# Keeping K's partial sums in PSUM over the whole first stage, and projecting B of the first SSD groups behind it

## The chip, the cores and the metric

The kernel runs on one core of one Trainium2 chip. The metric is the device time of one execution in microseconds. A time is given as the median of several runs; 0.2% of this kernel's time is 3.5 us.

Five engines matter: PE (TensorE, the matrix products), ACT (ScalarE), DVE (VectorE), POOL (GpSimd) and SP, whose queue here does nothing but start DMA transfers. Each engine takes its instructions strictly in the order of its own queue. An instruction that waits holds up all that stand behind it on its engine. PE writes its results into eight PSUM banks of 128x512 fp32.

## The reference

Two layers of a diffusion backbone on 256 latent tokens and 256 context tokens of width 2048. The even layer, with which the program starts:

```python
shift, scale, gate = adaln(c, ada_w[i], ada_b[i])              # silu(c) @ w + b
h  = modulate(rms_norm(x, norm_g[i]), shift, scale)            # h * (1 + scale) + shift
hc = modulate(rms_norm(ctx, norm_g[i]), shift_c, scale_c)      # the same with c_ctx
p  = h @ w_in                    # columns Q, gate G, Z, K, V, X, B, C, dt
pc = hc @ w_in[:, base:]         # of the context only K, V, X, B, C, dt
ya = neighbourhood_attention(q, k, v, k_ctx, v_ctx, rpb) * silu(gate)
yb = gated_group_rmsnorm(bidirectional_ssd(x, B, C, dt) + d * x, z, ssm_norm_g)
x  = x + gate * (concat([ya, yb]) @ w_out)
```

The odd layer is a gated short convolution between two projections. All products have fp32 accuracy: an operand is split into a high part (hH of the activations, H of a weight) and the low rest (hL, L), both rounded for the fast product type, and each product is three: hH·H, hL·H, hH·L.

## The kernel before, in words

The kernel is built by a Python program that writes all instructions in one order of its own. `Plan` keeps a modelled time for each engine. Pieces of work are Python generators that `spawn` puts into one of three lists (urgent, side, back); `pump` is called between the products of a stage and lets such a piece emit its next instructions when its inputs are modelled as ready; `force` emits pieces until a condition holds. So a change of buffers changes the order on all engines, and the hardware then runs each engine's queue in exactly that order.

**The first stage** (`for j in range(8)`) works through the contraction of 2048 in eight blocks j of 256. For block j it needs h of these rows, which needs the norm of x (row tiles 0 to 3: two of latent, two of context tokens, held in `x0` to `x3`), its transposes (`xm0` to `xm15`, two for each block, through a PSUM bank), and adaLN of the block: `A` (part 0, scale) and `S` (part 1, shift). A part is four loads of 0.5 MB from `ada0` and 16 small products (32x256); in blocks 4, 5 and 7 part 1 is made by DVE dot products instead (`csb<-raw,full`). From A, S and xm come `hH` on ACT (line 780) and `hL` on DVE (lines 786 and 792).

With h(j) the stage projects the first four heads: K (4 row tiles x 2 x 3 = 24 products), V (24), Q (2 row tiles, 12), each 128x512; and B of the first two SSD groups (12 products, into `psB0`). Q and B add up in PSUM over all eight blocks (2 + 2 banks). K and V don't: each row tile of each block gets a bank for six products and then `part_gen` takes it out, by an ACT copy in block 0 (line 816) and a DVE add into SBUF later (line 818): K into `gt` and `sz` (`parK`), V into `Vt`.

In block 0 the row tiles come one after another, since x arrives so: K, V and Q of tiles 0 and 1, then K and V of tile 2, then K and V of tile 3. `h(0, 3)` is the first block's h for tile 3, and needs the transposes of x3.

**Weights** come through five staging places `raw0` to `raw4` (and `PT`, `xtm`, `yi`, idle memory in this stage). A load is issued on SP by `issue` as soon as a place is free, in the order of `loads`. `split` then makes the high part on ACT (`w0` to `w2`, or `wH`, line 422) and `low_part` the low one on DVE (line 429). There are three weight places; `splits_try` emits a cast when a place is free and the weights are modelled to be there at most 300 ns behind the engines' time.

After the stage come G and dt, and `do_ssd(0)`: C, X, Z of the first two groups, then the attention of the first heads and so on.

Of the kernel before, what the change touches and what calls it, by code (L numbers as in the profile page):

```python
# [9 lines left out]
F32R = mybir.dt.float32r  # L10
# [131 lines left out]
def kernel(ctx: ExitStack, tc, x, cx, ada0, w0, adaT, w_in, w_out, sc_in, sc_out, rpb, small, const,  # L142
# [12 lines left out]
    def st(shape, tag, dt=F32, name=None):  # L155
        return sb.tile(list(shape), dt, tag=tag, name=name or tag, bufs=1)
# [21 lines left out]
    sz, xtm, yi = st([128, 4, 256], "sz"), st([128, 2, 512], "xtm"), st([128, 4, 256], "yi")  # L178
    PTs = st([128, 2, 4, 256], "PT")
    PT = [PTs[:, k] for k in range(2)]  # L180

# [27 lines left out]
    def spawn(q, gen, tmps=0, halves=0, late=0):  # L209
        q.append(Task(gen, tmps, halves, late))  # L210
# [192 lines left out]
    def split():  # L403
        k = pos["split"]
# [74 lines left out]
    def used():  # L479
        pos["use"] += 1  # L480
        w = in_use.popleft()
        if w is not None:
            free_w.append(w)
        splits_try()


# [318 lines left out]
    statk, statq = st([128, 16], "statk"), st([128, 8], "statq")  # L805


    szf, gtf = sz.rearrange("p a b -> p (a b)"), gt.rearrange("p a b -> p (a b)")
    parK = [szf[:, 0:512], szf[:, 512:1024], gtf[:, 0:512], gtf[:, 512:1024]]
    parV = [Vt[:, t, :] for t in range(4)]  # L810

    def part_gen(j, key, t, o, p):
# [107 lines left out]
            mm(ps, hH[kb][:, tt], HLo[1][:, k], False, last and k == 1)  # L920
            pump()

    pars = {"K": parK, "V": parV}

    def kv(j, key, t, HLo):
# [4 lines left out]
    def b_part(j):  # L930
        H, Lo = use()
        for k in range(2):
            mm_ws(psB0, hH[2 * j + k], hL[2 * j + k], H[:, k], Lo[:, k], 512, j == 0 and k == 0, j == 7 and k == 1)
        used()

    for j in range(8):
        need[0] = j
        if j == 1:
            plan.RATE = 360.0
        force(lambda: ("h", j, 0 if j == 0 else 3) in got, (urgent,) if j == 0 else (urgent, side))  # L940
        if j == 0:

            w3 = [use(k) for k in range(3)]
            psQ = banks(2)
            psk = banks(2)
            for k in range(2):

                for i, (a_, w_) in enumerate(((hH, 0), (hL, 0), (hH, 1))):
                    for t in range(2):
                        mm(psk[t], a_[k][:, t * 128:(t + 1) * 128], w3[0][w_][:, k], k == 0 and i == 0, k == 1 and i == 2)  # L950
            for t in range(2):
                spawn(urgent, part_gen(j, "K", t, parK[t], psk[t]))
            pump()
            for t in range(2):
                kv(j, "V", t, w3[1])
            for t in range(2):
                rows_(j, "Q", t, psQ[t], w3[2], True, False)
            for t in range(2, 4):
                force(lambda: ("h", j, t) in got, (urgent,))
                if t == 3:  # L960

                    free_w.append(in_use[2])
                    in_use[2] = None
                    splits_try()
                for key, k in (("K", 0), ("V", 1)):
                    kv(j, key, t, w3[k])
            for k in range(3):
                used()
            psB0 = banks(2)
            b_part(j)  # L970
        else:
            for key in "KVQ":
                HLo = use()
                for t in range(2 if key == "Q" else 4):
                    if key == "Q":
                        rows_(j, key, t, psQ[t], HLo, False, j == 7)
                    else:
                        kv(j, key, t, HLo)
                used()
            b_part(j)  # L980
    force(lambda: all(("part", 7, key, t) in got for key in "KV" for t in range(4)), (urgent,))
    plan.RATE = Plan.RATE
    KT, KL = st([128, 4, 512], "KT", F32R), st([128, 4, 512], "KL", F32R)


    cwh = st([128, 160], "cwh")
# [628 lines left out]

    Btm[0] = st([128, 2, 4, 128], "Btm", name="Btmt")
    spawn(urgent, first_v())
    spawn(urgent, kq_gen("K", 0, parK, 4, statk, KT, KL, False), 4)
    spawn(urgent, kq_gen("Q", 0, psQ, 2, statq, QT, QL, True), 2)

    def do_g(a, nxt, leave=False):
        psG = banks(2)
        proj(512, 256, psG, nxt, leave)
        spawn(urgent, silu2_gen("G", a, psG, gt, lambda: attn[0] >= 8 * a and (a or ("K", 0) in got)), 1)

    def do_ssd(s, nxt):
        if s:
            psB = banks(2)
            proj(256, 512, psB, 1)
            spawn(urgent, make_b(s, psB), 3)  # L1630
        psC, = banks(1)
        proj(256, 256, [psC], 4)
        spawn(urgent, make_c(s, psC), 0, 2)
        psX = banks(4)
        proj(512, 512, psX, 2)
        for gi in range(2):
# [3 lines left out]
        spawn(urgent, silu2_gen("Z", s, psZ, sz, lambda: ssd_done[0] >= 2 * s and ("K", 0) in got), 1)  # L1640
# [580 lines left out]
```

## Time and profile before

| | |
|---|---|
| runs | 1739.43, 1741.1, 1741.53 us; median 1741.1 |
| profiled execution | span 1738.3 us; its own time is not listed apart, and the three runs lie 1.1 to 3.2 us above this span |
| PE busy | 1717.7 us (99%) |
| weight loads into PE (PEld) | 1451.5 us (84%), beside the products |
| DVE busy | 1253.3 us (72%) |
| ACT busy | 776.2 us (45%) |
| granted PE clock | 9 tenths or more in all slices |
| memory traffic | 391.03 MB, mean 225 GB/s |
| first product of block 0 to 7 on K | 23.06, 52.73, 76.45, 95.09, 114.28, 133.45, 156.26, 173.90 us |
| end of the stage | about 190.4 us |

How to read it: a kernel whose PE is busy for 99% of the span gains only by fewer products or by fewer of the few waits that are left; it loses by each microsecond that PE stands. The first stage is where DMA is dense: its first three slices of 43 us move 375, 366 and 319 GB/s. In the lists below, "idle before <- X" or "X <- Y: a, b, c" says that work on X stood for a us in total, b times, c us at the longest, until Y was done. In a list in order of time, the first number is the start and the second the length, and "x2" two such instructions, which overlap.

### The profile page before, as it was taken

How to read it: one execution, taken by the hardware profiler on the slowest of the kernel's cores; microseconds unless marked ns; L12 is line 12 of the kernel's file. 1: busy time of each engine (PE TensorE's matmuls, PEld its weight loads, DVE VectorE, ACT ScalarE, POOL GpSimd, SP SyncE). 2: the span in 40 equal slices, each digit the busy share in tenths (PEclk: the TensorE clock that was granted, in tenths of full speed). 3: DMA queues.
4: the chain of work that ended last, by engine and by line, in shares of the span. 5: the costliest groups of instructions: out<-in, count | busy, mean ns of one | idle time of the engine just before them, and what ended most of it. 6: DMA issues, size and time to landing. Idle time of an engine off the chain costs nothing.

```text
span 1738.3 us, 24820 instructions
## 1 busy us (share of the span) xinstructions
PE 1717.7 (99%) x9255; PEld 1451.5 (84%) x9255; DVE 1253.3 (72%) x2108; ACT 776.2 (45%) x1367; POOL 33.2 (2%) x28
## 2 busy tenths in 40 slices
PE   6999999999999999999999999999999999999999
PEld 4777989889888889888888898888888888888887
DVE  5698787877576877676877687887668667665654
ACT  6434544445243445243435243665445344444442
POOL 0000100001000001000000000000000000000000
PEclk9999999999999999999999999999999999999999
DMA  9987644566754765755766567767867888776763
GB/s 375 366 319 271 206 135 142 180 209 187 228 183 151 234 210 183 227 188 164 230 221 195 191 196 248 258 225 254 280 204 260 267 272 284 246 241 191 248 213 114
DMA packets 192391, 391.03 MB, mean 225 GB/s; under 512 B 16200, under 2 KB 45960, under 8 KB 192016
## 3 DMA queue, kind: packets, MB, share of 16 engines
q1 hardware_dynamic: 184960, 382.88, 67.8%
q10 hardware_dynamic: 7312, 6.59, 1.2%
q8 instruction: 72, 1.18, 0.3%
q14 instruction: 47, 0.39, 0.1%
HBM read 379.79 MB, written 9.62 MB: 224 GB/s over the span
## 4 chain that ended last, share of the span: by engine, by line
PE 96%; DMA 2%; DVE 2%; issue 0%; SPq 0%; ACT 0%; POOL 0%; DVEq 0%; ACTq 0%
PE bank L196 93%; PE bank L200 3%; DMA raw<-in_ada 1%; DMA full<-dram_crow 1%; DVE csb L859 0%; DVE w L429 0%; DVE raw L859 0%; SPq L603 0%; DVE gt L818 0%; DVE yi L859 0%; DVE tmp L623 0%; DVE hL L792 0%; DVE sz L818 0%; DVE tmp L2116 0%; SPq L383 0%
## 5 line engine op out<-in xcount | busy, mean ns | idle before, releaser
L422 ACT CAST w<-raw 128x1024 fp32r<-128x1024 f32 (+1 forms) x344 | 359.8, 1047 | 554.7 <-PE bank L196 462.0
L429 DVE TENSOR_TENSOR w<-raw,w 128x1024 fp32r<-128x1024 f32 (+1 forms) x344 | 417.2, 1216 | 239.5 <-ACT w L422 238.2
L196 PE MATMUL bank<-hH,w 128*128 128x256 f32 (+1 forms) x2064 | 487.0, 325 | 0.0
L196 PE MATMUL bank<-w,hH 128*128 128x512 f32 x1280 | 405.7, 396 | 4.0 <-ACT hH L780 2.5
L196 PEld LDWEIGHTS bank<-hH,w 128*128 128x128 f32 x2064 | 345.3, 188 | 32.1 <-issue 1.7
L196 PE MATMUL bank<-hL,w 128*128 128x256 f32 (+1 forms) x1040 | 335.0, 322 | 0.0
L196 PEld LDWEIGHTS bank<-w,hH 128*128 128x128 f32 x1280 | 237.1, 188 | 56.3 <-DVE gt L818 3.4
L196 PE MATMUL bank<-w,hL 128*128 128x512 f32 x640 | 250.0, 391 | 0.2
L196 PEld LDWEIGHTS bank<-hL,w 128*128 128x128 f32 x1040 | 196.5, 189 | 14.5
L196 PE MATMUL bank<-w,h 128*128 128x512 f32 x768 | 178.2, 390 | 0.0
L196 PEld LDWEIGHTS bank<-w,h 128*128 128x128 f32 x768 | 144.1, 188 | 29.7
L888 DVE CUSTOM_DVE_ANT_0 raw<-raw,csb 128x1024 f32<-128x1024 f32 x128 | 155.3, 1218 | 11.9 <-DMA raw<-in_adaT 9.1
L196 PEld LDWEIGHTS bank<-w,hL 128*128 128x128 f32 x640 | 120.2, 188 | 25.7 <-DVE hL L792 0.9
L196 PE MATMUL bank<-w,mix 128*128 128x512 f32 x588 | 137.8, 391 | 0.0
L196 PEld LDWEIGHTS bank<-w,mix 128*128 128x128 f32 x588 | 109.7, 188 | 22.2 <-issue 0.3
L1371 DVE SCALAR_TENSOR_TENSOR tmp<-bank,cwh,tmp 128x508 f32<-128x508 f32 (+1 forms) x96 | 71.3, 746 | 1.9
L196 PE MATMUL bank<-KL,h 128*128 128x512 f32 x264 | 63.9, 390 | 0.0
L196 PEld LDWEIGHTS bank<-KL,h 128*128 128x128 f32 x264 | 49.5, 188 | 10.2
L196 PE MATMUL bank<-wH,h 128*128 128x512 f32 x168 | 55.7, 391 | 0.0
L196 PE MATMUL bank<-QT,h 128*128 128x512 f32 x168 | 55.7, 391 | 0.0
L429 DVE TENSOR_TENSOR wL<-raw,wH 128x1024 fp32r<-128x1024 f32 x31 | 37.9, 1223 | 23.9 <-ACT wH L422 23.8
L429 DVE TENSOR_TENSOR QL<-raw,QT 128x1024 fp32r<-128x1024 f32 x32 | 39.1, 1223 | 22.1 <-ACT QT L422 21.8
(306 smaller groups left out, 1962.3 us busy)
## 6 DMA issues: line engine op xcount, KB each, us to landing
raw<-in_w_in SPq DMA_DIRECT2D x196, 512.0 KB, 3.8
raw<-in_adaT SPq DMA_DIRECT2D x128, 512.0 KB, 4.8
raw<-in_sc_in SPq DMA_DIRECT2D x128, 512.0 KB, 4.7
raw<-in_w_out SPq DMA_DIRECT2D x64, 512.0 KB, 4.5
raw<-in_ada SPq DMA_DIRECT2D x35, 512.0 KB, 7.7
raw<-in_sc_out SPq DMA_DIRECT2D x32, 512.0 KB, 4.7
raw<-in_w SPq DMA_DIRECT2D x16, 512.0 KB, 5.5
tmp<-dram_csr SPq DMA_DIRECT2D x32, 256.0 KB, 5.2
```

The source lines that it names most:

```text
L196: E(T.matmul(o, l, r, start=start, stop=stop, skip_group_check=True))
L200: E(T.transpose(o, i, ident if k == 128 else ident[:k, :k]))
L422: E(S.copy(H, v))
L429: E(V.tensor_tensor(out=Lo, in0=v, in1=H.bitcast(F32), op=ALU.subtract))
L888: E(V.tensor_tensor_reduce(out=raw, in0=raw, in1=csb, scale=1.0, scalar=0.0, op0=ALU.mult, op1=ALU.add, accum_out=gp[:, h, m:m + 1]))
L1371: E(V.scalar_tensor_tensor(out=do, in0=di, scalar=cwh[:, 32 * k + ch:32 * k + ch + 1], in1=do, op0=ALU.mult, op1=ALU.add))
```

## The change

1. K gets four PSUM banks (`psK`) for the whole stage, its products add up there over all blocks; no copies, no adds. `kq_gen("K", ...)` later reads the banks.
2. That leaves two banks for V's partial sums (still taken out block by block), adaLN and the transposes of x; `psB0` no longer exists.
3. B is not projected in the stage. `do_ssd(0)` projects it as all later groups' B, from loads in full size (four of 0.5 MB instead of eight of 0.25 MB).
4. The memory of `gt` and `sz` is free until the stage ends and becomes a fourth weight place `wH3`/`wL3`, for the first 24 splits.
5. From block 1 on, K and V are projected row tile by row tile in turn, not K whole and then V.

```diff
-    QT, Vt, gt = st([128, 4, 256], "QT", F32R), st([128, 4, 512], "Vt"), st([128, 4, 256], "gt")
+    QT, Vt = st([128, 4, 256], "QT", F32R), st([128, 4, 512], "Vt")
+    WH.append(st([128, 1024], "gt", F32R, name="wH3"))
...
+    WL.append(st([128, 1024], "sz", F32R, name="wL3"))
...
-    free_w, in_use = deque(range(NW)), deque()
+    free_w, in_use = deque(range(NW + 1)), deque()
+    NFIRSTW = 24
+
+    def free_place():
+        return next((w for w in free_w if w != NW or pos["split"] < NFIRSTW), None)
 
     def place():
-        in_use.append(free_w.popleft())
-        return in_use[-1]
+        w = free_place()
+        free_w.remove(w)
+        in_use.append(w)
+        return w
...
-        while free_w and pos["split"] in RAW:
+        while free_place() is not None and pos["split"] in RAW:
...
-    weight(w_in, 0, 2, COL_B, 256)
...
-        weight(w_in, j * 256, 2, COL_B, 256)
...
-    for j_ in ssd_cols(0)[1:]:
+    for j_ in ssd_cols(0):
...
+    psK = []
+
+    def v_rows(j, t, HLo):
         ps, = banks(1)
-        rows_(j, key, t, ps, HLo, True, True)
-        spawn(urgent, part_gen(j, key, t, pars[key][t], ps))
+        rows_(j, "V", t, ps, HLo, True, True)
+        spawn(urgent, part_gen(j, "V", t, parV[t], ps))
+
+    def k_rows(j, t, HLo):
+        if j == 0:
+            psK.extend(banks(1))
+        rows_(j, "K", t, psK[t], HLo, j == 0, j == 7)
...
-            psB0 = banks(2)
-            b_part(j)
         else:
...
-            b_part(j)
+            HK = use()
+            for t in range(4):
+                k_rows(j, t, HK)
+                if t == 0:
+                    HV = use(1)
+                v_rows(j, t, HV)
+            used()
+            used()
+            HQ = use()
+            for t in range(2):
+                rows_(j, "Q", t, psQ[t], HQ, False, j == 7)
+            used()
...
-    spawn(urgent, kq_gen("K", 0, parK, 4, statk, KT, KL, False), 4)
+    spawn(urgent, kq_gen("K", 0, psK, 4, statk, KT, KL, True), 4)
...
     def do_ssd(s, nxt):
-        if s:
-            psB = banks(2)
-            proj(256, 512, psB, 1)
-            spawn(urgent, make_b(s, psB), 3)
+        psB = banks(2)
+        proj(256, 512, psB, 1)
+        spawn(urgent, make_b(s, psB), 3)
...
-    spawn(urgent, make_b(0, psB0), 3)
```

Over the whole program PE has 8849 matrix instructions in the order before and after. SP has 833 loads and stores instead of 837, DVE 28 adds (K) fewer, ACT four copies fewer.

The change also moves the order at the end of block 0, where row tile 3 is made ready. In the lists, a row is an instruction, by line, operation, output and inputs, and shape; numbers behind names are buffer numbers; line numbers after the change are higher by up to 8. On ACT, from the scaling of x3 on, before:

```order
L633 ACTIVATE x3_199<-x3_199,rx_153 128x512 x2
L816 COPY Vt_100<-bank7_89 128x512
L648 COPY xm0_137<-bank3_85 128x128
L648 COPY xm2_139<-bank1_83 128x256
L780 ACTIVATE hH0_297<-xm0_137,S0_155,A0_154 128x128
L780 ACTIVATE hH1_304<-xm1_138,S0_155,A0_154 128x128
L747 COPY half2_76<-bank0_82 128x256
```

and after:

```order
L641 ACTIVATE x3_199<-x3_199,rx_153 128x512 x2
L822 COPY Vt_100<-bank0_82 128x512
L430 CAST wH3_101<-raw1_91 128x1024
L656 COPY xm0_137<-bank3_85 128x128
L656 COPY xm2_139<-bank2_84 128x256
L656 COPY xm4_141<-bank0_82 128x256
L788 ACTIVATE hH0_297<-xm0_137,S0_155,A0_154 128x128
L788 ACTIVATE hH1_304<-xm1_138,S0_155,A0_154 128x128
L755 COPY half2_76<-bank2_84 128x256
```

The cast of block 1's K weights has come ahead of the copy of x3's transposes; before, the cast `w0_95<-raw3_93` of the same weights stood sixteen rows behind that copy.

On SP, the loads behind the constants, before (`in_w_in` is B of block 0, `in_ada0` adaLN, `in_w0` the K and V weights of block 1):

```order
L385 DMA raw2_92<-in_w_in 128x2x256
L383 DMA raw3_93<-in_ada0 128x1024
L383 DMA raw4_94<-in_ada0 128x1024
L383 DMA PT_107<-in_ada0 128x1024
L383 DMA xtm_105<-in_ada0 128x1024
L383 DMA yi_106<-in_ada0 128x1024
L383 DMA PT_107<-in_ada0 128x1024
L383 DMA raw0_90<-in_ada0 128x1024
L383 DMA raw1_91<-in_ada0 128x1024
L383 DMA raw3_93<-in_w0 128x1024
L383 DMA raw4_94<-in_w0 128x1024
```

and after:

```order
L385 DMA raw2_92<-in_ada0 128x1024
L385 DMA raw3_93<-in_ada0 128x1024
L385 DMA raw4_94<-in_ada0 128x1024
L385 DMA PT_107<-in_ada0 128x1024
L385 DMA xtm_105<-in_ada0 128x1024
L385 DMA yi_106<-in_ada0 128x1024
L385 DMA PT_107<-in_ada0 128x1024
L385 DMA raw0_90<-in_ada0 128x1024
L385 DMA raw1_91<-in_w0 128x1024 x2
L385 DMA raw2_92<-in_ada0 128x1024
```

B's load is gone and each adaLN load has moved to another place; the K and V weights of block 1 both go into raw1, where V's waits until K's is split.

On PE, behind the first transposes of x3 (`cpad` marks adaLN products, and the first rows of each list are transposes), before:

```order
L200 MATMUL bank1_83<-const_110,x2_196 128x128
L200 MATMUL bank1_83<-const_110,x3_199 128x128
L196 MATMUL bank0_82<-raw3_93,cpad_112 32x256 x4
L196 MATMUL bank0_82<-raw4_94,cpad_112 32x256 x4
L196 MATMUL bank0_82<-PT_107,cpad_112 32x256 x4
L196 MATMUL bank0_82<-xtm_105,cpad_112 32x256 x4
```

and after:

```order
L202 MATMUL bank0_82<-const_110,x2_196 128x128
L202 MATMUL bank0_82<-const_110,x3_199 128x128
L198 MATMUL bank3_85<-w0_95,hH0_297 128x512
L198 MATMUL bank3_85<-w0_95,hL0_301 128x512
L198 MATMUL bank3_85<-w0_95,hH0_297 128x512
L198 MATMUL bank2_84<-raw2_92,cpad_112 32x256 x4
L198 MATMUL bank2_84<-raw3_93,cpad_112 32x256 x4
```

The first three K products of row tile 3, which need hH0 and hL0 of h(0, 3), have come ahead of block 1's adaLN products.

More of the change, by code (lines that the diff above doesn't have):

```diff
@@ L483, in used @@
             free_w.append(w)
+        if pos["use"] == NFIRSTW:
+            free_w.remove(NW)
         splits_try()
@@ L805 @@
     statk, statq = st([128, 16], "statk"), st([128, 8], "statq")
-    szf, gtf = sz.rearrange("p a b -> p (a b)"), gt.rearrange("p a b -> p (a b)")
-    parK = [szf[:, 0:512], szf[:, 512:1024], gtf[:, 0:512], gtf[:, 512:1024]]
     parV = [Vt[:, t, :] for t in range(4)]
@@ L921, in rows_ @@
             pump()
-    pars = {"K": parK, "V": parV}
-    def kv(j, key, t, HLo):
+    psK = []
+    def v_rows(j, t, HLo):
         ps, = banks(1)
-        rows_(j, key, t, ps, HLo, True, True)
-        spawn(urgent, part_gen(j, key, t, pars[key][t], ps))
[L930 to L934, printed above, removed]
+        rows_(j, "V", t, ps, HLo, True, True)
[4 more added lines that the diff above has]
+        rows_(j, "K", t, psK[t], HLo, j == 0, j == 7)
     for j in range(8):
@@ L944 @@
             psQ = banks(2)
-            psk = banks(2)
+            psK += banks(2)
             for k in range(2):
@@ L949 @@
                     for t in range(2):
-                        mm(psk[t], a_[k][:, t * 128:(t + 1) * 128], w3[0][w_][:, k], k == 0 and i == 0, k == 1 and i == 2)
-            for t in range(2):
-                spawn(urgent, part_gen(j, "K", t, parK[t], psk[t]))
+                        mm(psK[t], a_[k][:, t * 128:(t + 1) * 128], w3[0][w_][:, k], k == 0 and i == 0, False)
             pump()
             for t in range(2):
-                kv(j, "V", t, w3[1])
+                v_rows(j, t, w3[1])
             for t in range(2):
@@ L964 @@
                     splits_try()
-                for key, k in (("K", 0), ("V", 1)):
-                    kv(j, key, t, w3[k])
+                k_rows(j, t, w3[0])
+                v_rows(j, t, w3[1])
             for k in range(3):
                 used()
-            psB0 = banks(2)
-            b_part(j)
-        else:
[L972 to L979, printed above, removed]
-            b_part(j)
-    force(lambda: all(("part", 7, key, t) in got for key in "KV" for t in range(4)), (urgent,))
+        else:
+            HK = use()
[10 more added lines that the diff above has]
+            used()
+    force(lambda: all(("part", 7, "V", t) in got for t in range(4)), (urgent,))
     plan.RATE = Plan.RATE
     KT, KL = st([128, 4, 512], "KT", F32R), st([128, 4, 512], "KL", F32R)
+    gt, sz = st([128, 4, 256], "gt"), st([128, 4, 256], "sz")
     cwh = st([128, 160], "cwh")
@@ L1623, in do_g @@
         proj(512, 256, psG, nxt, leave)
-        spawn(urgent, silu2_gen("G", a, psG, gt, lambda: attn[0] >= 8 * a and (a or ("K", 0) in got)), 1)
+        spawn(urgent, silu2_gen("G", a, psG, gt, lambda: attn[0] >= 8 * a), 1)
     def do_ssd(s, nxt):
-        if s:
-            psB = banks(2)
-            proj(256, 512, psB, 1)
-            spawn(urgent, make_b(s, psB), 3)
+        psB = banks(2)
+        proj(256, 512, psB, 1)
+        spawn(urgent, make_b(s, psB), 3)
         psC, = banks(1)
@@ L1639, in do_ssd @@
         proj(512, 256, psZ, nxt)
-        spawn(urgent, silu2_gen("Z", s, psZ, sz, lambda: ssd_done[0] >= 2 * s and ("K", 0) in got), 1)
+        spawn(urgent, silu2_gen("Z", s, psZ, sz, lambda: ssd_done[0] >= 2 * s), 1)
         for gi in range(2):
             spawn(side, group_gen(s, gi), 4, 4, 3000)
-    spawn(urgent, make_b(0, psB0), 3)
     do_g(0, 1)
```

2 lines of the change are left out of this document (1 added, 1 removed).

## The prediction, as put on record before the changed kernel ran

> **What bounds the kernel now.** I read the page's busy line and chain first, then the windows, then the waits of TensorE (PE) inside the first stage, 23.06 us (first product) to 190.4 us.
>
> ```profile
> PE 1717.7 (99%) x9255; PEld 1451.5 (84%) x9255; DVE 1253.3 (72%) x2108; ACT 776.2 (45%) x1367; POOL 33.2 (2%) x28
> PE 96%; DMA 2%; DVE 2%; issue 0%; SPq 0%; ACT 0%; POOL 0%; DVEq 0%; ACTq 0%
> ...
> 0.00:20.00 20.00, 8.92 (x86) 5.91 (x90) 9.90 (x33) 10.09 (x23) 1.31 (x6) 1.00 0.91 351
> 20.00:40.00 20.00, 16.65 (x112) 11.00 (x101) 13.87 (x37) 14.97 (x32) 1.98 (x4) 1.00 1.04 400
> 40.00:60.00 20.00, 20.00 (x172) 14.24 (x173) 11.51 (x28) 9.01 (x20) 0.00 (x0) 1.00 0.96 358
> 23.06:190.40 167.34, 163.59 (x984) 122.65 (x985) 129.91 (x236) 74.56 (x132) 1.98 (x4) 1.00 0.86 312
> ...
> PE bank L196 <- ACT hH L780: 2.5, 2, 1.4
> PE bank L196 <- DVE gt L818: 1.5, 3, 0.7
> PE bank L200 <- ACT half L747: 0.4, 1, 0.4
> PE bank L200 <- ACT x L633: 0.3, 1, 0.3
> ```
>
> PE works 1717.7 of 1738.3 us and carries 96% of the chain. A window's row gives length, then busy us of PE, weight loads, DVE, ACT and POOL, granted clock, DMA share, GB/s. In the stage PE lacks 3.75 of 167.34 us; the waits name 4.7 us, nearly all that any edit of the stage could give back. And to 60 us the stage lives on a full memory path: 351, 400, 358 GB/s.
>
> **The change part by part.** *PE.* The number of products is the same. What a product costs is read from a stretch without waits:
>
> ```profile
> 80.42 0.62 PE L196 MATMUL bank<-w,hH 128*128 128x512 f32 x2
> 80.87 0.39 PE L196 MATMUL bank<-w,hL 128*128 128x512 f32 x1
> 81.10 0.62 PE L196 MATMUL bank<-w,hH 128*128 128x512 f32 x2
> ```
>
> Three products from 80.42 to 81.10: 0.227 us each, three 0.68. B's 12 products a block are 2.72 us, 8 blocks 21.8 us. They leave the stage and come back whole in do_ssd(0), in the same stationary form. PE waits nowhere there that the list shows, so this is 0 on the path; what it does is take 2.72 us of cover out of each block. Bounds: 1.0 better (every B transition free) to 2.7 worse (one block's B not hidden behind the weights' arrival); I take 0, the groups' rows are alike.
>
> *The adds of K.* They are 28 on DVE:
>
> ```profile
> L818 DVE TENSOR_TENSOR gt<-gt,bank 128x512 f32<-128x512 f32 x14 | 9.5, 682 | 0.7 <-PE bank L196 0.7
> L818 DVE TENSOR_TENSOR sz<-sz,bank 128x512 f32<-128x512 f32 x14 | 9.2, 683 | 2.1 <-PE bank L196 2.0
> L859 DVE CUSTOM_DVE_ANT_0 csb<-raw,full 128x1024 f32<-128x1024 f32 x7 | 8.5, 1220 | 0.9 <-DMA raw<-in_ada 0.9
> ```
>
> 18.7 us of DVE work and four ACT copies go, off the path except for the 1.5 us that PE waited on adds into gt. With the 0.4 us on a half copy I count 1.9 us back (between 0 and 4.7, all waits listed). What may replace them are V's adds: with K and Q parked in six banks only two banks turn over, and an add now may stand behind dot products (1220 ns each); that is a rival below.
>
> *The splits of B.* Eight half-size casts and low parts become four whole ones, eight loads of 0.26 MB four of 0.52 MB, all on the same queues, later. The page's GB/s by slices of 43 us, as far as the place where B now stands (the fifth and after):
>
> ```profile
> GB/s 375 366 319 271 206 135 142 180 209 187 228 183 151 234 210 183 227 188 164 230 221 195 191 196 248 258 225 254 280 204 260 267 272 284 246 241 191 248 213 114
> ```
>
> 206, 135 and 142 where 400 was reached earlier: room for two more loads, ACT and DVE likewise. I take 0; bounds 0.3 better (the half copy's waits go) and 1.4 worse (the longest wait of the list, for a cast instead of hH).
>
> *The fourth weight place and SP's queue.* This decides. The order under the change shows ACT's row: CAST wH3<-raw1, the first half of block 1's K weights, stands in front of the copy xm0<-bank3 that takes row tile 3's transposes from PE. On SP its load is row 26, behind the eight adaLN loads of block 1. What the queues did then:
>
> ```profile
> 21.94 0.38 SPq L385 DMA_DIRECT2D raw<-in_w_in  x1
> 24.83 2.72 SPq L383 DMA_DIRECT2D raw<-in_ada  x2
> 31.60 1.61 SPq L383 DMA_DIRECT2D raw<-in_ada  x2
> 38.75 0.80 SPq L383 DMA_DIRECT2D raw<-in_w  x2
> ...
> GB/s 412 402 412 410 410 410 410 410 399 398 398 423 399 430 399 430 379 430 389 440 379 430 410 338 225 113 369 399 440 379 461 369 410 399 399 430 410 410 430 389
> ...
> DMA to landing us min/median/max: 4.3/6.8/7.6
> ```
>
> (SP's issues; the GB/s of 30 to 46 us in slices of 0.4; the landings of line L383 from 24 to 46 us, of which the least, 4.3, is K1's: issued 38.75, landed 43.05.) K1 was issued only when PE had freed raw3 at 38.7, and the memory path ran dry meanwhile: 338, 225, 113 GB/s from 39.2 to 40.4, which is 1.65 slices' worth, so all that was issued ahead ended near 39.2 + 1.65 x 0.4 = 39.9. In the changed kernel K1 goes to raw1, free early, and follows the adaLN loads without the gap; B's 0.26 MB is not ahead of it (0.26/0.41 = -0.6), its own 0.52 MB is (+1.3): last byte at 40.5. Before, the path picked up at 40.4 and K1's landing came 2.6 later for 1.3 us of bytes, so 1.3 more: 41.8. I take 41.5, bounds 40.5 and 42.4. Now ACT and DVE there:
>
> ```profile
> 36.47 1.34 ACT L633 ACTIVATE x<-x,rx 128x512 f32<-128x512 f32 x2 [0.27 <-POOL rx L592]
> 37.72 0.56 ACT L816 COPY Vt<-bank 128x512 f32<-128x512 f32 x1
> 38.18 0.54 ACT L648 COPY xm<-bank 128x128 f32<-128x128 f32 x2
> 38.60 0.89 ACT L780 ACTIVATE hH<-xm,S,A 128x128 fp32r<-128x128 f32 x2
> ...
> 48.68 2.00 ACT L422 CAST w<-raw 128x1024 fp32r<-128x1024 f32 x2
> ...
> 38.48 0.70 DVE L649 COPY xm<-bank 128x128 f32<-128x128 f32 x2 [0.49 <-ACT xm L648]
> 39.09 0.34 DVE L786 TENSOR_SCALAR tmp<-xm,A,S 128x128 f32<-128x128 f32 x1
> 39.54 0.29 DVE L792 TENSOR_TENSOR hL<-tmp,hH 128x128 fp32r<-128x128 f32 x1
> 49.76 2.36 DVE L429 TENSOR_TENSOR w<-raw,w 128x1024 fp32r<-128x1024 f32 x2
> ```
>
> ACT is through with Vt at 38.2 and now stands until 41.5. The cast takes 1.05 (2.00 for two, overlapping), so xm0 is copied from 42.55 instead of 38.18, xm2 and xm4 follow, and hH0 is there at 43.9. DVE copies xm1, xm3, xm5 after ACT's copies, then does the low part of K1 (1.2, half of 2.36) ahead of row tile 3's: hL0 at 45.6. Queued on PE behind hH0 are the products that follow, in order:
>
> ```profile
> 37.25 0.88 PE L200 MATMUL bank<-const,x 128*128 128x128 f32 x6 [0.30 <-ACT x L633]
> 38.05 1.07 PE L196 MATMUL bank<-raw,cpad 128*32 128x256 f32 x16
> 50.87 0.64 PE L196 MATMUL bank<-PT,cpad 128*32 128x256 f32 x8
> 52.73 0.50 PE L196 MATMUL bank<-w,hH 128*128 128x512 f32 x1
> ```
>
> Before, PE went from the transposes straight into adaLN of block 1 (38.05), which needs nobody but DMA. Now the first three K products of tile 3 stand ahead of it, and the transposes have two more pairs: they end near 38.7. PE then waits
>
> - for hH0 from 38.7 to 43.8: 5.1;
> - for hL0 from 44.1 to 45.6: 1.5;
> - at V of tile 3, whose bank holds xm8: ACT, 4.4 late, has hH1, two half copies, xm6 and V's cast (1.05) ahead of that copy: 1.0;
> - at the first K products of block 1: DVE has V's low part (1.2) ahead of the sums S from which hH2 and hL2 are made: 1.1.
>
> Sum 8.7 us, in a stretch where it waited for nothing (20.00 of 20 busy). Bounds: with K1 at 40.5 the first wait is 4.1 and the last two may vanish, 5.6 in all; with 42.4 it is 6.0 and 9.6. I take 8.7, since adaLN work (1.86 a part, 50.87 to 52.73) no longer lies in the gap. It can't be given back: block 1 on is PE at 99%.
>
> **Sum**: 1738.3 + 8.7 - 1.9 + 0 = 1745.1 us of span. The runs lie 1.1 to 3.2 above the profiled span, their median 2.8; 1745.1 + 2.8 = 1747.9, so 1748.0, or +6.9.
>
> [...] At the start of the program the same transposes run at two speeds (rows from 10 to 14.1 us, and from 14.3 to 16.8):
>
> ```profile
> L200 PE MATMUL bank<-const,x 128*128 128x128 f32 x7 | 1.7, 421 | 0.0
> L200 PE MATMUL bank<-const,x 128*128 128x128 f32 x25 | 3.0, 276 | 0.0
> ```
>
> 421 ns and then 276, 1.7/7 = 0.24 us against 3.0/25 = 0.12 of busy time each. A cold PE is thus half as fast here, though the granted clock reads 1.00. A second cold start after the 5.1 us wait would double the products of the next 3.7 us (first PE work near 10.5 to 14.2) and cost 1.9. [...]
>
> **Rivals.** *Faster*: K1 lands before ACT asks. ACT asks at 38.2, so 3.3 us earlier than I have it; then no wait arises and the listed ones go: 1741.1 - 1.9 = 1739, at best 1741.1 - 4.7 = 1736.4. Against it: the path is at 400 GB/s from 20 to 40, it would have to carry 3.3 x 0.41 = 1.35 MB more, and only B's 0.26 MB was taken off. It decides at a landing of 38.2 and is half gone at 40.
>
> *About the same*: K1 lands at 40.5 or sooner and the last two waits are absorbed by the work around them: PE's waits 5.6, less 1.9, and less up to 2.8 if the rest of the listed waits goes too: +0.9 to +3.7, some 1743.
>
> *Two banks*: V's add waits behind three dot products and a split on DVE: 3 x 1.22 + 1.22 + 0.68 = 5.6 us, while PE, with two banks, can go on for V, K, V products, 3 x 1.37 = 4.1: 1.5 us lost at each such place, three to six of them: +4.5 to +9 on my sum, 1752 to 1757. For it: DVE is 129.91 of 167.34 busy. Against: 18.7 us of that goes away with K's adds.
>
> *Cold clock*: +1.9 on the sum, 1749.9.
>
> That the change doesn't move what it says is excluded: the order shows the adds gone and B's products behind the stage.
>
> **How the numbers follow.** Forecast 0.50; cold clock 0.12; two banks 0.13; about the same 0.17; faster 0.08. Slower is the first three, 0.75. 0.2% is 3.5 us, about what the runs (2.1 us apart) can tell from nothing. 1740 to 1754 leaves out the faster case (0.08), a little of the same case, and a third of the two-bank case.
>
> **What would show it.** ACT idle some 3.3 us near 38 for a load of raw<-in_w; PE's waits on line L788 (hH) grow from 2.5 to about 7, and there is a PE gap of 5 us at 38.7; adds of V alone, 28, and none into gt or sz; block 1's first K product near 55.7 instead of 52.73; the stage's end, now without B, near 190.4 - 21.8 + 6.8 = 175.4. I am wrong if ACT's cast of wH3 starts before 39.5, if PE's wait there is under 3 us, or if waits on the V adds come to over 3 us.

## The result: 14.6 us slower, and the profile after

The changed kernel took 1754.39 to 1756.76 us, median 1754.9, against 1739.43 to 1741.53, median 1740.3, for the kernel before in the same sessions. The ratio is 1.0086, 95% interval 1.0074 to 1.0098. The direction was forecast, the +6.9 was about half of it, and 1754.9 lies above the range of 1740 to 1754. The profiled execution has a span of 1752.6 us and a time of 1754.39, so times stand 1.8 above spans; the difference of the profiled spans is 14.3.

The page's first lines, and PE's waits from 23 to 200 us:

```profile
PE 1721.2 (98%) x9255; PEld 1451.4 (83%) x9255; DVE 1237.1 (71%) x2076; ACT 773.9 (44%) x1359; POOL 31.4 (2%) x28
...
PE bank L198 <- ACT hH L788: 6.7, 3, 4.2
PE bank L198 <- DVE hL L800: 1.8, 2, 1.1
PE bank L198 <- DVE Vt L824: 1.1, 1, 1.1
PE bank L198 <- DVE A L763: 1.0, 1, 1.0
PE bank L198 <- DVE xm L657: 0.9, 1, 0.9
PE bank L202 <- ACT half L755: 0.5, 1, 0.5
PE bank L198 <- DVE wL L437: 0.3, 1, 0.3
```

In the stage, up to Q's last product, PE's idle time went from 3.75 to 11.33 us. The wait for gt is gone, as it must be; the wait for hH grew from 2.5 to 6.7, and five that were not there came: for hL, for V's adds, for adaLN's sums (A), for xm and for the low part of a weight, 5.1 us together. ACT and PE at the place that the prediction spoke of:

```profile
39.19 0.56 ACT L822 COPY Vt<-bank 128x512 f32<-128x512 f32 x1
42.47 1.04 ACT L430 CAST wH<-raw 128x1024 fp32r<-128x1024 f32 x1 [2.73 <-DMA raw<-in_w]
43.42 0.81 ACT L656 COPY xm<-bank 128x128 f32<-128x128 f32 x3
44.11 0.89 ACT L788 ACTIVATE hH<-xm,S,A 128x128 fp32r<-128x128 f32 x2
...
39.80 0.66 PE L202 MATMUL bank<-const,x 128*128 128x128 f32 x4 [0.20 <-ACT Vt L822]
44.67 0.79 PE L198 MATMUL bank<-w,hH 128*128 128x512 f32 x1 [4.22 <-ACT hH L788]
46.58 0.80 PE L198 MATMUL bank<-w,hL 128*128 128x512 f32 x1 [1.12 <-DVE hL L800]
47.74 2.79 PE L198 MATMUL bank<-raw,cpad 128*32 128x256 f32 x24
56.09 0.50 PE L198 MATMUL bank<-w,hH 128*128 128x512 f32 x1 [0.92 <-DVE xm L657]
58.37 0.50 PE L198 MATMUL bank<-wH,hH 128*128 128x512 f32 x1
59.58 0.50 PE L198 MATMUL bank<-wH,hL 128*128 128x512 f32 x1 [0.72 <-DVE hL L800]
```

ACT stands 2.73 us for K1's load, then casts, then copies x3's transposes; PE stands 4.22 us for hH, 1.12 for hL, 0.92 for xm8's bank, and 0.72 for hL behind block 1's first K product. These four were forecast at 5.1, 1.5, 1.0 and 1.1. That first K product starts at 58.37, forecast near 55.7. And 24 adaLN products from 47.74 on take 2.79 us; by the prediction's row of 16 in 1.07 they would take some 1.6. The windows say why. They are cut at the points where the granted clock changes; the number behind POOL's is the clock:

```profile
40.52:43.93 3.41, 0.00 (x0) 0.00 (x0) 0.21 (x1) 1.46 (x4) 0.00 (x0) 1.00 0.06 25
43.93:47.34 3.41, 1.55 (x3) 0.79 (x3) 3.05 (x8) 1.07 (x4) 0.00 (x0) 0.50 0.12 37
47.34:50.76 3.42, 3.42 (x34) 1.39 (x32) 0.00 (x0) 0.00 (x0) 0.00 (x0) 0.50 0.55 204
50.76:54.17 3.41, 3.41 (x45) 2.09 (x41) 0.92 (x4) 1.69 (x3) 0.00 (x0) 1.00 0.83 243
```

Behind a window without a product the clock is 0.50 for two windows of 3.41 us. And far behind the stage, in the output projection, PE waits twice where it had waited for nothing (ACT, then PE):

```profile
1146.24 0.37 ACT L1258 COPY half<-bank 128x256 f32<-128x256 f32 x1 [2.77 <-PE bank L198]
1148.47 2.94 ACT L430 CAST w<-raw 128x1024 fp32r<-128x1024 f32 x3
...
1149.56 0.49 PE L198 MATMUL bank<-w,mix 128*128 128x512 f32 x1 [1.68 <-ACT w L430]
1150.82 2.57 PE L198 MATMUL bank<-w,mix 128*128 128x512 f32 x10 [0.77 <-DVE w L437]
```

Three casts of w_out stand on ACT behind a copy that waits for the attention's products; PE waits 2.4 us.

The account of the profiled spans: first product 23.06 to 24.52, +1.5; idle time in the stage +7.6; halved clock, by the busy time in its two windows, at most (1.55 + 3.42)/2 = 2.5; idle time in the tail +2.4. Sum 14.0 of 14.3. The first product's 1.5 is not the change's: before_tail below, whose program is the same up to there as the kernel before, had it at 24.60. How much of it stands in the medians is not shown.

### The profile page after: what moved, and what is told of

The parts are those of the page before. It is cut to its first block, busy times and chain, and to the rows that moved or that the text cites. A ratio compares the mean times of both kernels' runs of the same rounds, so it can differ in the third digit from the quotient of the medians.

```text
span 1752.6 us, 24755 instructions
## 1 busy us (share of the span) xinstructions
PE 1721.2 (98%) x9255; PEld 1451.4 (83%) x9255; DVE 1237.1 (71%) x2076; ACT 773.9 (44%) x1359; POOL 31.4 (2%) x28
## 4 chain that ended last, share of the span: by engine, by line
PE 95%; DMA 2%; DVE 2%; ACT 1%; issue 0%; SPq 0%; DVEq 0%; ACTq 0%
PE bank L198 92%; PE bank L202 3%; DMA full<-dram_crow 1%; DMA raw<-in_ada 0%; DVE csb L865 0%; DMA raw<-in_w 0%; DMA xtm<-in_w 0%; DVE w L437 0%; ACT hH L788 0%; DVE wL L437 0%; DVE Vt L824 0%; DVE hL L800 0%; ACT wH L430 0%; SPq L611 0%; ACT w L430 0%
## 5 line engine op out<-in xcount | busy, mean ns | idle before, releaser
L437 DVE TENSOR_TENSOR w<-raw,w 128x1024 fp32r<-128x1024 f32 x340 | 414.5, 1222 | 263.8 <-ACT w L430 258.1
L430 ACT CAST w<-raw 128x1024 fp32r<-128x1024 f32 x340 | 357.5, 1053 | 545.9 <-PE bank L198 477.6
L198 PE MATMUL bank<-w,hH 128*128 128x512 f32 x1200 | 382.4, 396 | 9.7 <-ACT hH L788 6.7
L198 PEld LDWEIGHTS bank<-w,hH 128*128 128x128 f32 x1200 | 222.1, 188 | 57.5 <-ACT hH L788 7.4
L198 PE MATMUL bank<-w,hL 128*128 128x512 f32 x600 | 234.3, 391 | 1.2 <-DVE hL L800 1.1
L198 PEld LDWEIGHTS bank<-hL,w 128*128 128x128 f32 x1040 | 196.2, 189 | 14.6
L198 PEld LDWEIGHTS bank<-w,hL 128*128 128x128 f32 x600 | 112.7, 188 | 25.4 <-DVE hL L800 2.2
L437 DVE TENSOR_TENSOR wL<-raw,wH 128x1024 fp32r<-128x1024 f32 x35 | 42.8, 1222 | 23.6 <-ACT wH L430 23.6
L430 ACT CAST wH<-raw 128x1024 fp32r<-128x1024 f32 x36 | 37.9, 1052 | 45.3 <-PE bank L198 34.6
L437 DVE TENSOR_TENSOR QL<-raw,QT 128x1024 fp32r<-128x1024 f32 x32 | 39.1, 1223 | 24.8 <-ACT QT L430 24.7
L198 PE MATMUL bank<-wH,h 128*128 128x512 f32 x168 | 55.7, 390 | 0.0
```

The costliest lines, as they stand in the source:

```text
L198: E(T.matmul(o, l, r, start=start, stop=stop, skip_group_check=True))
L430: E(S.copy(H, v))
L437: E(V.tensor_tensor(out=Lo, in0=v, in1=H.bitcast(F32), op=ALU.subtract))
```

## The experiments

Theory 1: the early cast on ACT, with its load behind a full memory path, is the price. Theory 2: two working banks are. Theory 3: B's products were cover (work of PE during which other engines get ready what PE needs next), and moving them costs.

**late_place.** The fourth place is given only when h(0, 3) is done, so that the cast stands behind hH1 on ACT.

```diff
-        return next((w for w in free_w if w != NW or pos["split"] < NFIRSTW), None)
+        return next((w for w in free_w if w != NW or (("h", 0, 3) in got and pos["split"] < NFIRSTW)), None)
```

> The changed kernel, but the fourth weight place may be used only once h of row tile 3 in block 0 is written. Theory 1 (the early cast of block 1's K weights on ACT, ahead of x3's copies, is the price): PE's gap of 4.2 us near 40 and the waits for hL behind it go, the clock stays at 1.00 from 24 to 58 us, and of the 14.6 us lost 8 to 11 come back: 1744 to 1747. Theory 2 (two working banks, and V's adds, are the price): the waits move but stay, 1753 to 1756. In both cases the 2.5 us of waits near 1149 may go or stay, since the order there may change again.

1750.6 us (ratio to before 1.0057, interval 1.0042 to 1.0072): 4.3 back, not 8 to 11, between the ranges of the two theories. Idle time in the stage is 7.57, the 4.2 us gap is gone. ACT still stands 1.77 us for the same load and begins the cast at 42.53, as late as before; but hH0 and hH1 are now made ahead of it. Yet the clock is not clean, as two windows of late_place show:

```profile
50.45:53.86 3.41, 1.91 (x16) 0.90 (x19) 2.85 (x8) 2.54 (x5) 0.00 (x0) 1.00 0.99 376
53.86:57.27 3.41, 3.41 (x31) 1.88 (x22) 0.10 (x1) 0.37 (x1) 0.00 (x0) 0.50 1.03 417
```

No long gap stands here, only waits of 0.8 and 0.7 us near each other; PE is busy 56% of the first window and pays for the second, 3.41/2 = 1.7 us. So theory 1 holds for the gap and explains under a third of the loss.

**no_fourth.** No fourth place at all.

```diff
-    free_w, in_use = deque(range(NW + 1)), deque()
-    NFIRSTW = 24
+    free_w, in_use = deque(range(NW)), deque()
+    NFIRSTW = 0
```

> The changed kernel without the fourth weight place (three, as before the change); K in four banks and B behind the stage are kept. Theory 1: the cast can't come early since no place is free, so as with the place given late, 1744 to 1748, a little slower than that if the fourth place helps to prepare weights. Theory 2: as the changed kernel or slower, 1754 to 1758.

1759.0 us (1.0107, 1.0092 to 1.0122), outside both ranges. The gap near 40 is gone here too, but three places are too few: PE waits for hL 3.7 us in four places (1.7 and 1.0 of them at the start of block 5), for low parts of weights 1.9 (two places behind the stage), and has two windows of halved clock from 130.9 (mean 0.97 from 60 to 190 us) and one more near 1155. Between this and late_place lie 8.5 us: the fourth place is worth having, if it isn't taken too early.

**b_behind.** The kernel before, with B alone moved.

```diff
-    weight(w_in, 0, 2, COL_B, 256)
...
-        weight(w_in, j * 256, 2, COL_B, 256)
...
-            psB0 = banks(2)
-            b_part(j)
...
-        if s:
-            psB = banks(2)
-            proj(256, 512, psB, 1)
-            spawn(urgent, make_b(s, psB), 3)
+        psB = banks(2)
+        proj(256, 512, psB, 1)
+        spawn(urgent, make_b(s, psB), 3)
```

> The kernel before with one part of the change alone: B of the first groups projected behind the stage; K is summed in SBUF as before, with four working banks. Theory 1: moving B costs nothing by itself, 1739 to 1742. Theory 3 (B's products were cover for the weights and the adds, so that moving them costs): 1744 or more, with new waits of PE between 53 and 190 us.

1767.7 us (1.0156, 1.0141 to 1.0171): 28 us slower, as theory 3 has it. Its waits in the stage, the window from 60 to 190, and the chain ahead of block 4 (two rows of DVE, one of ACT, two of PE):

```profile
PE bank L196 <- ACT hH L778: 7.2, 5, 1.7
PE bank L196 <- DVE hL L790: 7.2, 5, 1.9
PE bank L196 <- DVE w L429: 2.6, 1, 2.6
...
60.00:190.00 130.00, 117.49 (x638) 87.18 (x639) 98.56 (x166) 47.35 (x76) 0.00 (x0) 0.92 0.76 277
...
107.40 1.21 DVE L857 CUSTOM_DVE_ANT_0 xtm<-xtm,full 128x1024 f32<-128x1024 f32 x1
108.66 0.16 DVE L866 TENSOR_REDUCE S<-statk 128x4 f32<-128x8 f32 x1
109.05 0.60 ACT L778 ACTIVATE hH<-xm,S,A 128x256 fp32r<-128x256 f32 x1 [4.75 <-DVE S L867]
109.70 0.50 PE L196 MATMUL bank<-w,hH 128*128 128x512 f32 x1 [1.69 <-ACT hH L778]
112.08 0.79 PE L196 MATMUL bank<-w,hL 128*128 128x512 f32 x1 [1.88 <-DVE hL L790]
```

DVE's list shows no wait from 87.6 to 112 us: adds, low parts and dot products fill it. Block 4's last dot product ends at 108.6; S, hH and PE's first product follow from there, and hL comes behind two more dot products, of a later block. PE waits for hH and hL in this way at the starts of blocks 4, 5 and 7, the three with dot products, and windows of halved clock stand behind each of these clusters: the mean clock in the row from 60 to 190 us is 0.92. Another window of halved clock stands at 53.8 us, behind the wait of 2.6 us for a weight's low part. In all 23.9 us of the stage have the halved clock, which by the busy time in them costs up to 11.0. With 13.1 us more idle time in the stage, waits of 2.8 behind it and a first product 1.2 later this accounts for the 27.7 between the two profiled spans.

**b_behind_no_dots.** As b_behind, with `DOTS = ()`: adaLN's second part of these blocks goes to PE. Its weights still lie in the layout made for dot products, so the shifts of blocks 4, 5 and 7 are not the reference's; the work is that of the other blocks.

```diff
-    DOTS = (4, 5, 7)
+    DOTS = ()
...
-        yield when(lambda: ("S", DOTS[-1]) in got)
+        yield when(lambda: need[0] >= 7)
...
-    spawn(side, dot_gen())
```

> As b_behind (K summed in SBUF, B behind the stage), but part 1 of adaLN of blocks 4, 5 and 7 is made by PE like the others instead of by dot products on DVE. If B's products were cover for DVE (adds of K and V and dot products together), the waits at the starts of blocks 4, 5 and 7 and the halved clock behind them go (11 us of waits, 10 of clock), and PE has 3 x 1.9 us more to do: 1750 to 1756. If B covered something else (weights, memory): within 5 us of b_behind, 1763 to 1773.

1751.2 us (1.0057, 1.0042 to 1.0072), 16.6 faster than b_behind. The waits for hL are gone and hH's are those of the kernel before:

```profile
PE bank L196 <- ACT hH L778: 2.5, 2, 1.4
PE bank L196 <- DMA raw<-in_ada: 1.9, 4, 0.6
PE bank L196 <- DVE w L429: 2.6, 1, 2.6
```

The clock stays at 1.00 through the stage (1.000 in the mean of the whole profile). So B's 2.7 us a block were cover for DVE's work, above all where the dot products stand. The run takes work from DVE and gives PE 5.7 us more at once, so it doesn't say what either does alone. The 2.6 us for a weight's low part stay; with PE's added work and 3.3 us of waits for adaLN's loads they are most of the 10.6 us that are left over the kernel before.

In the changed kernel no wait stands at the starts of these blocks. Two differences say what pays for the cover. no_fourth differs from b_behind only in K's half of the change (sums in banks, no adds, two working banks, row tiles in turn) and is 8.7 us faster, though it still waits 2.7 us at the start of block 5; late_place adds the fourth place and is 8.5 faster again. The gain of both is spent on the cover that went. No run has the 28 adds of K alone.

**k_then_v.** late_place without the interleaving.

```diff
             for t in range(4):
                 k_rows(j, t, HK)
-                if t == 0:
-                    HV = use(1)
+            used()
+            HV = use()
+            for t in range(4):
                 v_rows(j, t, HV)
             used()
-            used()
```

> As late_place, with the interleaving undone: from block 1 on K of all four row tiles, then V of all four. If two working banks are what V's adds wait for (theory 2), four V tiles in a row need a bank each 1.37 us and PE waits for Vt adds or xm copies grow by 3 to 10 us: 1753 to 1760. If not, within 2 us of late_place: 1749 to 1752.

1758.5 us (1.0102, 1.0086 to 1.0117), 7.9 slower than late_place. The waits that grew:

```profile
PE bank L198 <- DVE Vt L824: 3.4, 3, 2.1
PE bank L198 <- DVE hL L800: 2.0, 3, 1.0
```

Idle time in the stage is 12.22 us, 4.7 more than in late_place. Five windows of the profiled execution, the slowest of four, have the halved clock in the stage (mean clock of the whole profile 0.995), against one in late_place (0.998). Two of these, at 24.7 and 41.8 us, lie ahead of the edit and are not its doing; two are new, in blocks 4 and 5. By the profiles the edit costs 4.7 us of idle time and up to 3.4 of halved clock. So two banks do bind, theory 2's mechanism, and the interleaving keeps most of it away.

**k1_first.** The changed kernel with K1's load ahead of adaLN's.

```diff
+    w_seg(1, CK)
     q_ada(1)
...
-        w_seg(j, CK, CV)
+        w_seg(j, *((CV,) if j == 1 else (CK, CV)))
```

> The changed kernel with one load moved: the K weights of block 1 ahead of the eight adaLN loads of block 1 instead of behind them. The cast on ACT can then be early without standing, and the order of PE has adaLN of block 1 ahead of row tile 3 again. Theory 1 (the load behind a full memory path is what made the early cast cost): the 4.2 us gap and the halved clock behind it go, 1745 to 1750, at or below late_place. If the loss were in K's banks or in B's absence, it stays above 1752.

1754.4 us (1.0078, 1.0063 to 1.0093), no gain clear of the scatter, where 1745 to 1750 was expected. The order then put the cast still earlier, ahead of ACT's work on x2 (ACT, then PE):

```profile
32.34 1.05 ACT L430 CAST wH<-raw 128x1024 fp32r<-128x1024 f32 x1 [5.44 <-DMA raw<-in_w]
...
37.75 0.69 PE L202 MATMUL bank<-const,x 128*128 128x128 f32 x2 [4.75 <-ACT x L642]
```

ACT stands 5.44 us on the same cast, PE 4.75. The load was issued at 22.35 and its cast began at 32.34. The same mechanism, one row tile sooner: the earlier load didn't help here, since the free place let the cast ask for it sooner still.

**warm.** The changed kernel with 18 products of zeros on PE in the 4.2 us gap.

```diff
+    zero = st([128, 64], "zero", F32R)
+    nc.vector.memset(zero.bitcast(F32), 0.0)
...
+                if t == 3:
+                    for _ in range(18):
+                        T.matmul(psQ[0][0:64, :], zero, w3[0][0][:, 0], start=False, stop=False, skip_group_check=True)
                 k_rows(j, t, w3[0])
```

> The changed kernel with 18 more products with a zero stationary operand (64 columns, added to a Q bank, so 0 is added) placed on PE where it stands idle for 4.2 us; all else as it was. If the halved clock from 44 to 51 us (granted clock 0.50) comes from that idle time, it stays at 1.00 and the adaLN products there take 1.9 us instead of 3.4: 1.5 us less, about 1753.4. If the clock isn't a price of its own: 1754.9, or more by what the filling overruns.

1754.9 us (1.0082, 1.0065 to 1.0098), no gain in time. The windows:

```profile
43.78:47.19 3.41, 1.82 (x10) 0.66 (x12) 3.04 (x8) 1.06 (x4) 0.00 (x0) 1.00 0.11 20
47.19:50.60 3.41, 3.41 (x32) 1.36 (x32) 0.00 (x0) 0.00 (x0) 0.00 (x0) 0.50 0.73 269
```

One of the two windows is cured; the wait for hL (1.42 here) leaves PE busy 53% of the next and the adaLN products run at a clock of 0.50 as before. For the clock's price in time this run settles nothing.

**late_tail.** late_place, with casts allowed earlier in the order from the output projection on.

```diff
-            if plan.ready([RAW[pos["split"]][1]]) > max(plan.t["PE"], plan.t["ACT"]) + 300:
+            if plan.ready([RAW[pos["split"]][1]]) > max(plan.t["PE"], plan.t["ACT"]) + (300 if plan.t["PE"] < 1100e3 else 900):
```

> As late_place, and from the output projection on a weight cast may be put in the order up to 900 ns, not 300, ahead of the modelled arrival of its load. That puts the casts of w_out which stood behind an attention copy and three mix casts on ACT (near 1147 us) ahead of them. If that order is the cause of the 2.4 us that PE waits there, and of the halved clock that follows in some runs, the wait goes: 2.4 to 4.2 us faster than late_place (1750.6), 1746.4 to 1748.2. If the data come late there, the wait stays.

1746.4 us (1.0034, 1.0021 to 1.0046), 4.1 faster than late_place. Idle time behind the stage falls from 2.96 to 0.54 us, which is the kernel before's 0.52, and the halved clock near 1146 is gone.

**after_tail** is the same edit on the changed kernel, **before_tail** on the kernel before.

> The changed kernel with only the later order edited as in late_tail (casts up to 900 ns ahead from the output projection on). If the wait near 1149 us is a term of its own and adds up with the early cast: the 2.4 us of waits go and the halved clock behind them where it fell, 1754.9 - 2.4 to 4.2 = 1750.7 to 1752.5. If late_tail's gain needed the late place: 1754 or more.

> The kernel before with the same edit of the later order. It had no wait of PE there, so there is nothing to gain: 1739 to 1742. If it gets faster by 2 us or more, the edit is a gain of its own and late_tail doesn't show a cost of the change.

**after_tail**: 1751.1 us (1.0061, 1.0046 to 1.0076), 3.8 faster than the changed kernel. The term adds up with the cast: late_tail, which has both edits, is 4.7 faster than after_tail, much as late_place was 4.3 faster than the changed kernel. **before_tail**: the kernel before gets slower, 1745.7 (1.0027, 1.0016 to 1.0037), where 1739 to 1742 was expected. Its order changes too, and new waits come:

```profile
1190.43 0.73 PE L196 MATMUL bank<-w,mix 128*128 128x512 f32 x2 [1.77 <-ACT mix L1010]
1191.86 0.50 PE L196 MATMUL bank<-w,mix 128*128 128x512 f32 x1 [0.69 <-DVE mix L1012]
```

These waits are 2.5 of the 5.4 us; what the rest is was not taken apart. So the edit is no gain of its own. The tail's order is shaken by whatever is changed ahead of it, and a row of the new order may or may not leave 2.5 us of waits; the kernel before had one without. The first product of this run's profile is the 24.60 spoken of above.

**late_tail_warm.** late_tail with nine products of zeros in the three waits between 48 and 53 us.

```diff
+                if t == 3:
+                    for _ in range(3):
+                        T.matmul(psQ[0][0:64, :], zero, hH[0], start=False, stop=False, skip_group_check=True)
                 v_rows(j, t, w3[1])
...
+                if j == 1 and t == 0:
+                    for _ in range(3):
...
                 k_rows(j, t, HK)
...
             mm(ps, hH[kb][:, tt], HLo[0][:, k], first and k == 0, False)
+            if (j, key, t, k) == (1, "K", 0, 0):
...
```

> As late_tail, with nine products with a zero operand (0 is added to a Q bank) at the three places between 48 and 53 us where PE waits 0.9, 0.8 and 0.7 us. They lie in time that is lost anyway. If the halved clock of 53.6 to 57.0 us comes from the share of idle time in the 3.4 us before it (busy 0.56), it goes: 1.7 us less, about 1744.7. If the clock follows something else: 1746.4 or a little more.

1744.7 us (1.0023, 1.0014 to 1.0033): 1.7 faster than late_tail by doing nine products more. The runs of each of the two kernels scatter over some 3 us, so the medians alone are a rough price; but the profiles agree, where the first product behind the stage moves from 175.28 to 173.67 us, 1.6 sooner, with the stage's first product at 24.1 in both. The windows:

```profile
50.00:53.40 3.40, 3.28 (x19) 1.47 (x21) 2.83 (x9) 2.55 (x5) 0.00 (x0) 1.00 1.03 392
53.40:56.80 3.40, 3.39 (x44) 2.14 (x36) 1.05 (x4) 0.75 (x2) 0.00 (x0) 1.00 1.03 420
```

With PE busy through the first, the second is at 1.00 and gets through 44 products; late_place's got through 31.

**late_tail_sums.** The sums of block 1's shift ahead of V of row tile 3.

```diff
+                    got.add(("S1", j))
...
+                if t == 3:
+                    force(lambda: ("S1", 1) in got, (urgent,))
                 v_rows(j, t, w3[1])
```

> As late_tail, with the shift sums of block 1 (adaLN part 1) put in the order ahead of V of row tile 3, so that V's products lie in the time in which hH and hL of block 1 are made. If the waits of 0.9, 0.8 and 0.7 us there are an order in which PE asks too early, most of the 2.4 us and the 1.7 us of halved clock go: 1742 to 1744.5. If they come from two banks being too few, they come back in the next blocks: 1745.5 to 1748.

1754.0 us (1.0073, 1.0058 to 1.0088), worse than either theory had it. Block 1's first K products wait for nothing now but hL (0.9), and the loss comes elsewhere. Its waits, in the profile of its fastest execution (1749.65; the others took 1753.8 to 1755.5):

```profile
PE bank L198 <- DVE hL L801: 3.5, 4, 1.3
PE bank L198 <- DVE w L437: 1.7, 1, 1.7
```

Waits for hL go from 0.9 to 3.5 us, the wait for a weight's low part is new (near 410 us, behind the stage), and a halved window stands at 131, in block 5.

## Why the prediction was wrong, step by step

None of the three signs that the prediction had named for being wrong came: the cast of wH3 started at 42.47 us, not before 39.5, PE's wait there was 4.22, not under 3, and waits on V's adds came to 1.1, not over 3. The error lies mostly in terms that it held at 0. The spans were to differ by 6.8 us and differ by 14.3; of the 7.5 between, the halved clock is up to 2.5, the waits of the tail 2.4, the first product 1.5 and idle time in the stage 0.8. The 2.8 us that it added from span to time compare different executions (within one it is 1.8 here); since both kernels have that step, the +6.9 does not rest on it.

**The early cast on ACT (8.7 us of waits): right in mechanism and place, its four waits slightly too dear.** They came to 4.22 + 1.12 + 0.92 + 0.72 = 7.0 us. The landing was forecast at 41.5; the cast began at 42.47 in a run whose first product was 1.46 late. Undoing it gave 4.3 us in the medians, because late_place keeps about half of these waits and one halved window.

**"1.9 us back" in the stage: failed.** The waits for gt went, but waits on V's adds (1.1), on adaLN's sums (1.0) and on a weight's low part (0.3) took their place. In all, 7.6 us of idle time came against the forecast's 8.7 - 1.9 = 6.8: the two errors nearly cancel, which is luck.

**The clock, left out of the sum: the first term that failed.** It was a rival at 1.9 us and 0.12, the author's estimate from the program's first products; that a wait in mid program slows PE again was shown by no row of before. The sum itself forecast such a wait, 5.1 us. The runs showed up to 2.5 us in the stage, more than the one cold start of the estimate, since the first halved window (PE busy 45%) was followed by another. late_tail_warm measures the price of one window by itself: 1.7. In the profile of after the clock is 0.50 behind the empty window from 40.52 to 43.93 us; in late_place it is 0.50 also behind a window in which PE was busy 56%.

**"B behind the stage: 0, bounds 1.0 better to 2.7 worse": failed as a price of that part alone.** b_behind shows 28 us. That the sum did not miss by as much is luck: K's half of the change, whose adds the prediction put "off the path", is worth 8.7 us and the fourth place, taken late, 8.5 once B is moved. With these, and with the cast, the tail and one halved window mended, 27.4 us over the kernel before (b_behind) become 4.4 (late_tail_warm). A loss of 28 us and gains of 17 stood in the sum as 0.

**Nothing behind the stage: another term that failed.** The sum took all work behind the stage as unchanged. The order of the output projection, a thousand microseconds later, changed with it: 2.4 us of waits, and 3.8 to 4.1 in the medians when they are taken out; behind them the clock is 0.50 from 1146.12 us in late_place's profile, and stays at 1.00 in after's.

**The rivals.** Faster and about the same were out: K1's cast began at 42.47, later than the 38.2 and 40.5 that they needed, by more than the 1.5 us of the late start. Two banks: the mechanism exists (k_then_v: 7.9 us), but the interleaving that is part of the change holds it to waits for Vt and xm of 2.0 us.

**The account from the experiments.** Of 1754.9, the early cast is 4.3, the tail's order 4.1 and the halved window near 54 us 1.7, each taken out by a run; 1744.7 is left. That is 4.4 above the 1740.3 of before. What is left is idle time in the stage, 7.66 us in late_tail against 3.75:

```profile
PE bank L198 <- ACT hH L788: 4.3, 4, 1.4
PE bank L198 <- DVE xm L657: 1.6, 3, 0.9
PE bank L198 <- DVE Vt L824: 1.2, 1, 1.2
PE bank L198 <- DVE hL L800: 0.9, 2, 0.7
```

xm and Vt are banks that are emptied too late, 2.8 us; the waits for hH are 1.8 more than before (2.5) and those for hL 0.9. Whether another order would remove them stays open: the one that was tried, late_tail_sums, moved them. No version that was run beats the kernel before.

## What to carry to other kernels

In a pipeline that is balanced to a per cent, work that looks idle in the sum may be cover: before PE work is moved out of a stage, look which engine is the next to bind there (DVE here, above all in three of eight blocks; 28 us for B's products), not whether PE waits now. A new buffer can let a producer come earlier in program order, and its engine then stands for the load (ACT 2.73 us here, 5.44 in k1_first); give the buffer a condition, not only a place. And when one program writes the order of the whole kernel, an edit at 40 us shifts the order at 1150 us: compare the waits of the whole trace, and take a few microseconds of waits far from the edit as part of its price.

## What the runs showed of the hardware

In the traces of before and after, each stretch of one granted clock lasts 3.4133 us or a multiple, up to the program's last few microseconds: in before 1723.73 us at 1.00 (505 times, from 14.19 us on); in after 27.31 us at 1.00 (8 times, from 16.62 us), 6.83 at 0.50 (2 times) and 1699.84 at 1.00 (498 times). Windows of 3.41 us from these two profiles and those of late_place and warm, by their start in us, with the clock of the window behind:

| window | its clock | PE busy | clock behind it |
|---|---|---|---|
| after, 40.52 | 1.00 | 0.00 | 0.50 |
| late_place, 1142.71 | 1.00 | 0.39 | 0.50 |
| after, 1146.44 | 1.00 | 0.51 | 1.00 |
| warm, 43.78 | 1.00 | 0.53 | 0.50 |
| late_place, 50.45 | 1.00 | 0.56 | 0.50 |
| before, 21.02 | 1.00 | 0.56 | 1.00 |
| before, 31.26 | 1.00 | 0.57 | 1.00 |
| after, 43.93 | 0.50 | 0.45 | 0.50 |
| after, 47.34 | 0.50 | 1.00 | 1.00 |
| late_place, 53.86 | 0.50 | 1.00 | 1.00 |

So the halved clock did not need an empty window here; between 0.51 and 0.56 both happened, and these rows don't say what decides. In after, 24 adaLN products take 2.79 us at 0.50 (from 47.74) and 1.50 at 1.00 (from 60.25). One halved window cost 1.7 us in the medians, the gain of late_tail_warm, so that in late_place two waits of 0.8 and 0.7 us next to each other cost as much again as they last.

At the program's start the transposes speed up where the trace's first record of a full clock begins. (Ahead of it the trace has none, and the 1.00 that a view prints there is no measured clock.) In before, where that is 14.19 us, they take 421 ns each from 10 to 14.1 us and 276 from 14.3 to 16.8; in after, where it is 16.62, still 415 from 14.3 to 16.5 and 278 from 16.7 on. All 32 take 4.42 us in before and 5.35 in after. That is 0.9 of the 1.46 us by which block 0's first product is later in after; most of the rest is the first adaLN product, which waits for its load until 10.47 in before and 11.02 in after.
